# A layer norm cut into two token halves, and modulation steps moved behind their weight tiles

## The chip, the cores and the metric

The kernel runs on one core of a Trainium2 chip. The metric is the device time of one execution in microseconds (us). All arithmetic is in float32; the projections are made of matmuls on two float32r parts of each operand.

## What is computed

Two groups of tokens, 512 of a denoising step and 128 of a context, pass through two layers that share their weights. The kernel keeps them side by side as T = 640 columns, with the 1024 features in 8 chunks of 128 partitions (`kc` 0 to 7).

```python
for l in range(DEPTH):                                   # 2 layers
    sh1, sc1, ga1, sh2, sc2, ga2 = split(silu(c) @ w_ada[l] + b_ada[l])
    h = rmsnorm(x, g_attn[l]) * (1 + sc1) + sh1
    z = h @ w_in[l]     # q, k, v | gq, gk, gv, gate | zf, zb
    o_na = neighbourhood_attention(q, k, v, cache_k, cache_v, rpb)   # or context attention
    o_gla = gla_bidir(rope(gq), rope(gk), gv, lf(zf), lb(zb), state_fwd, state_bwd)
    x = x + ga1 * (concat(o_na, rmsnorm(o_gla) * silu(gate)) @ w_o[l])
    h = rmsnorm(x, g_mlp[l]) * (1 + sc2) + sh2
    x = x + ga2 * (relu(h @ w_up[l]) ** 2 @ w_down[l])
```

## The kernel before

**Weights.** Each layer's projections are cut into weight units of 128 x 1024 (512 KB): 24 of `w_in`, one small `z`, 8 of `w_o`, 32 of `w_up`, 32 of `w_down` (`dn`). `unit_order` (L377) lists them in the order of use. `prefetch` (L418) transfers them ahead on the SP queue into three buffers `wr`; ACT then rounds a unit to its high part `wh` and POOL subtracts to get the low part `wl`, each in three buffers. A unit that stands twice within four places of the list has its subtraction shared between DVE and POOL. A tile is the product of one unit with all tokens: 8 chunks, three matmuls (`wh` with the high part of h, `wh` with the low, `wl` with the high) for each of the token halves 0 to 256 and 256 to 640 (`HALF`), so 48 matmuls.

**Modulation steps.** The six modulation vectors come from products with `w_ada`, a step for each vector and chunk: `ada_step` (L498) reads a 512 KB tile of `w_ada` and makes two DVE instructions (`junk<-wr,cbc` and `wr<-wr,cbc`), one for each group's condition. In the first attention half (layer one, `adab == 1`) there are 24 of them, in the same three `wr` buffers as the weights: one each with units 6 to 23 of `w_in`, six with the first four of `w_o` (`steps_at`). In the list a step's tile stands right behind the weights of its tile. `proj` calls the step after the first chunk of that tile, `proj4` after its last evacuation. These calls give the order in which instructions are written down, not the order on DVE.

**Order.** PE's order is that of the program, made by a planner (`Drv`) that interleaves the tiles with tasks of the attention: `gla_pair`, `gv_task`, `v_task`, `qk_task`, `na_unit`. The order on the other engines is made at compile time by a scheduler, which takes instructions by priority when it reckons their inputs to be ready. An instruction without early inputs, like a step's, can so be put far ahead of its place in the program.

**The GLA chain.** `gla_pair` runs once for each pair of heads. DVE makes decay factors (`ex`), states (`ST`), masked blocks (`Dg`, `A`); PE consumes each, and PE's fixed order waits at the first that is late.

**Norm of layer two.** Every norm but the first is late: `late_begin` and `late_chunk` (L749, L762) give the projection the rows G * x, without the factor rstd, and with two shift columns more (TX = 642). The sum of squares (`sqa`) is finished meanwhile (`late_stat`), and each evacuation multiplies by `lrstd` on DVE and adds the shift's product on ACT (`whole`, and the first branches of `gla_rope`, `v_task`). Between the layers, `mlp` (L1520) does this at b == 8 for the last four `dn` units, over all tokens at once; then `late_first` (L633) starts the first two tiles of layer two and the `z` tile. The first norm of layer one is a half-token norm instead (`norm_begin`, `norm_rstd`, `norm_out`, L697 on): for each half, rstd, product `y`, scale and shift, high part on ACT, low part on POOL (or DVE). Evacuations then need neither `lrstd` nor `whole`.

## Time and profile before

| | us |
|---|---|
| median of 3 runs | 1763.83 |
| lowest, highest | 1761.66, 1766.52 |
| profiled execution | 1761.31 |
| its span | 1759.5 |
| PE busy | 1654.6 (94%) |
| DVE busy | 1087.4 (62%) |
| ACT busy | 706.4 (40%) |
| POOL busy | 606.6 (34%) |

The span runs from the first instruction to the last of one execution; its own time is 1.8 us longer. Busy time of one engine overlaps that of the others. All instructions are made by one helper, so every row has line L197, and groups are told apart by tile names: `ps_mm` and `ps_sm` are PSUM accumulators, `row` is a row of x, h or an attention output. Layer one's attention half lies from 64 to 432 us, its second norm and MLP to 913, layer two's attention half to 1274, its MLP behind that.

### The profile page before, as it was taken

What the parts mean: (1) busy time and instruction counts of PE and PEld (TensorE: products, weight loads), DVE (VectorE), ACT (ScalarE), POOL (GpSimd) and SP (SyncE); (2) the same over time, 40 slices, a digit from 0 to 9 for tenths busy, and PEclk for the clock granted to TensorE, in tenths of its full rate; (3) what the DMA queues carried; (4) which work ended last, traced back from release to release, by engine and by line L of the source; (5) the groups of instructions that cost most, each with busy time, mean ns of one, the idle gap of its engine ahead of it and who ended that gap; (6) DMA issues with size and microseconds to landing.
All of it is one profiled execution on the core that took longest, in us unless ns stands there. A gap on an engine that the chain in (4) does not pass through costs nothing. (4 is left out here: it accounts for less than half of the span.)

```text
span 1759.5 us, 32558 instructions
## 1 busy us (share of the span) xinstructions
PE 1654.6 (94%) x13708; PEld 1579.8 (90%) x13708; DVE 1087.4 (62%) x1983; ACT 706.4 (40%) x1141; POOL 606.6 (34%) x249
## 2 busy tenths in 40 slices
PE   8977687999999999999998897999999999999999
PEld 6976677779999999999998796878899999999998
DVE  5787857786697787777666766478662222222322
ACT  4525325553543233322344364467355223332330
POOL 1243522122344444444434355313133333333331
PEclk9989889999999999999999998999999999999999
DMA  9222214241354453445231111222212222222221
GB/s 367 67 88 76 85 59 149 84 133 49 108 180 145 146 178 132 144 145 167 75 132 49 42 50 57 77 66 79 77 61 84 74 83 72 73 73 83 73 72 72
DMA packets 60770, 177.18 MB, mean 101 GB/s; under 512 B 6865, under 2 KB 17745, under 8 KB 60625
## 3 DMA queue, kind: packets, MB, share of 16 engines
q1 hardware_dynamic: 44784, 157.66, 26.7%
q10 hardware_dynamic: 15840, 17.45, 3.2%
q8 instruction: 108, 1.77, 0.4%
q14 instruction: 38, 0.30, 0.1%
HBM read 168.26 MB, written 6.82 MB: 100 GB/s over the span
## 5 line engine op out<-in xcount | busy, mean ns | idle before, releaser
L197 POOL TENSOR_TENSOR wl<-wr,wh 128x1024 fp32r<-128x1024 f32 x184 | 480.7, 2613 | 922.4 <-ACT wh L197 855.5
L197 PE MATMUL ps_mm<-row,wh 128*128 128x256 f32 x2416 | 485.0, 323 | 0.8 <-POOL row L197 0.7
L197 ACT ACTIVATE wh<-wr 128x1024 fp32r<-128x1024 f32 x191 | 202.1, 1058 | 597.2 <-PE ps_sm L197 401.6
L197 PEld LDWEIGHTS ps_mm<-row,wh 128*128 128x128 f32 x2416 | 402.3, 194 | 19.8 <-issue 12.5
L197 PE MATMUL ps_mm<-row,wl 128*128 128x256 f32 (+2 forms) x1208 | 282.2, 315 | 0.5 <-DVE wl L197 0.5
L197 PEld LDWEIGHTS ps_mm<-row,wl 128*128 128x128 f32 x1208 | 227.0, 194 | 0.7 <-DVE wl L197 0.7
L197 DVE SCALAR_TENSOR_TENSOR row<-ps_mm,mod,row 128x512 f32<-128x512 f32 (+1 forms) x176 | 88.6, 543 | 89.5 <-PE ps_mm L197 89.4
L197 DVE SCALAR_TENSOR_TENSOR row<-ps_sm,mod,row 128x256 f32<-128x256 f32 (+1 forms) x216 | 81.4, 431 | 95.7 <-PE ps_sm L197 95.7
L197 DVE SCALAR_TENSOR_TENSOR ar<-ar,cbc 128x1024 f32<-128x1024 f32 x56 | 122.2, 2189 | 0.7
L197 ACT ACTIVATE r<-r 128x640 f32<-128x640 f32 (+2 forms) x192 | 112.2, 617 | 18.5 <-DVE r L197 15.0
L197 PE MATMUL ps_sm<-row,wh 128*128 128x256 f32 (+1 forms) x624 | 119.2, 310 | 0.0
L197 PE MATMUL ps_sm<-uh,wl 128*128 128x256 f32 (+1 forms) x512 | 116.5, 309 | 0.0
L197 PE MATMUL ps_mm<-uh,wl 128*128 128x256 f32 (+1 forms) x512 | 116.4, 309 | 0.0
L197 PE MATMUL ps_mm<-ul,wh 128*128 128x256 f32 (+1 forms) x512 | 116.4, 309 | 0.0
L197 PE MATMUL ps_sm<-uh,wh 128*128 128x256 f32 (+1 forms) x512 | 116.4, 309 | 0.0
L197 PE MATMUL ps_sm<-ul,wh 128*128 128x256 f32 (+1 forms) x512 | 116.4, 309 | 0.0
L197 PE MATMUL ps_mm<-uh,wh 128*128 128x256 f32 (+1 forms) x512 | 116.3, 309 | 0.0
L197 DVE TENSOR_TENSOR ul<-r,uh 128x640 fp32r<-128x640 f32 x64 | 55.1, 861 | 84.5 <-ACT r L197 84.4
L197 DVE TENSOR_TENSOR r<-ps_mm,rstd 128x642 f32<-128x642 f32 x34 | 28.1, 826 | 123.7 <-PE ps_mm L197 123.7
L197 PEld LDWEIGHTS ps_sm<-row,wh 128*128 128x128 f32 x624 | 103.3, 189 | 0.0
L197 PE MATMUL ps_mm<-m,wh 128*128 128x256 f32 (+1 forms) x544 | 102.0, 309 | 0.0
L197 PEld LDWEIGHTS ps_sm<-uh,wl 128*128 128x128 f32 x512 | 93.3, 188 | 0.0
(214 smaller groups left out, 2947.0 us busy)
## 6 DMA issues: line engine op xcount, KB each, us to landing
wr<-w_up SPq DMA_DIRECT2D x64, 512.0 KB, 3.5
wr<-w_dn SPq DMA_DIRECT2D x64, 512.0 KB, 3.5
ar<-w_ada SPq DMA_DIRECT2D x56, 512.0 KB, 3.8
wr<-w_in SPq DMA_DIRECT2D x48, 512.0 KB, 3.6
wr<-w_ada SPq DMA_DIRECT2D x24, 512.0 KB, 3.5
wa<-w_ada SPq DMA_DIRECT2D x16, 512.0 KB, 10.2
wr<-w_o SPq DMA_DIRECT2D x16, 512.0 KB, 3.5
tab<-bias ACTq DMA_DIRECT2D x32, 96.0 KB, 2.1
```

The costliest lines, as they stand in the source:

```text
L197: r = f(*args, **kw)
```

## The change

Three things change.

- In the first attention half a modulation step is called behind the last evacuation of its tile, no longer after the first chunk, and both its instructions get an ordering edge to the last matmul written down so far (`lastmm`), so that the scheduler can't put them on DVE ahead of that point. The edge makes no wait on the chip.
- Layer two's first norm becomes a half-token norm. The last four `dn` units stand twice in the list; `norm_tail` runs them for tokens 0 to 256 and then for 256 to 640. After the first pass `norm_half_task` makes the first half's rows, beside the second pass. `first_a` runs layer two's first two tiles over the first half, `first_b` the `z` tile and the second half.
- Layer two's attention half has T = 640 columns and evacuates without `lrstd` and `whole` (`lateh` is False there). `z` moves behind the first two units in the list.

```diff
--- before.py
+++ after.py
@@ -385,7 +385,7 @@
                 u.append(("ada", *next(it)))
         for l in range(L):
             for i in range(24):
-                if i == (4 if l == 0 else 0):
+                if i == (4 if l == 0 else 2):
                     put("z", l, 0)
                 put("in", l, i)
             for i in range(4):
@@ -395,6 +395,9 @@
             for b in range(9):
                 for i in range(4 if b < 8 else 0):
                     put("up", l, 4 * b + i)
+                if b == 8 and l + 1 < L:
+                    for i in range(4):
+                        put("dn", l, 4 * (b - 1) + i)
                 for i in range(4 if b > 0 else 0):
                     put("dn", l, 4 * (b - 1) + i)
         assert next(it, None) is None
@@ -502,8 +505,12 @@
         ui, t = self.unit("ada", l, v, kc)
         junk = self.junk()
         for r in range(2):
-            nc.vector.scalar_tensor_tensor(out=junk if r == 0 else t, in0=t, scalar=1.0, in1=self.cbc[:, r], op0=ALU.mult,
+            i = nc.vector.scalar_tensor_tensor(out=junk if r == 0 else t, in0=t, scalar=1.0, in1=self.cbc[:, r], op0=ALU.mult,
                                            op1=ALU.mult, accum_out=self.mod[l][:, v, kc, r:r + 1])
+            if self.adab == 1:
+                self.tc.add_manual_dep(i.ins, self.lastmm.ins.name, mybir.DependencyInfo(
+                    mybir.DependencyClass.NoSync, mybir.DependencyReason.DATA), reason="order")
         if kc == KC - 1:
             b0 = PC_BADA + 48 * l + 8 * v
             m = self.mod[l][:, v]
@@ -543,22 +550,22 @@
         for i, (w, h) in enumerate(((wh, hh), (wh, hl), (wl, hh))):
             for hf in halves:
                 lo = self.HALF[hf][0]
-                nc.tensor.matmul(ps[0][hf], lhsT=w, rhs=h[:, lo:lo + ps[0][hf].free_size()],
+                self.lastmm = nc.tensor.matmul(ps[0][hf], lhsT=w, rhs=h[:, lo:lo + ps[0][hf].free_size()],
                                  start=first and i == 0 and (hf == 1 or shared is None),
                                  stop=last and i == 2 and (hf == 1 or shared in (None, 1)))
         self.dv.pe(sum((0.32, 0.48)[hf] for hf in halves))
 
-    def mmz(self, ps, w):
-        for kc in range(KC):
-            hh, hl = self.h[kc]
-            for m, h in ((64, hh), (32, hl)) if kc < KC - 1 else ((32, hl), (64, hh)):
-                for hf in range(2):
-                    lo = self.HALF[hf][0]
-                    self.nc.tensor.matmul(ps[0][hf][0:m], lhsT=w[:, kc, 0:m], rhs=h[:, lo:lo + ps[0][hf].free_size()],
+    def mmz(self, ps, w, halves=(0, 1)):
+        for hf in halves:
+            lo, hi = self.HALF[hf]
+            for kc in range(KC):
+                hh, hl = self.h[kc]
+                for m, h in ((64, hh), (32, hl)) if kc < KC - 1 else ((32, hl), (64, hh)):
+                    self.nc.tensor.matmul(ps[0][hf][0:m], lhsT=w[:, kc, 0:m], rhs=h[:, lo:hi],
                                           start=kc == 0 and m == 64, stop=kc == KC - 1 and m == 64)
-        self.dv.pe(4.7)
+            self.dv.pe((1.9, 2.8)[hf])
 
     def mmf(self, f, kc, halves, shared=None):
         ui, ps, w = f
@@ -594,7 +601,7 @@
         ps, nsm = self.acc_any(n=n)
         for kc in range(KC):
             self.mm3(ps, wh[:, kc], wl[:, kc], *self.h[kc], kc == 0, kc == KC - 1)
-            if kc == 0:
+            if kc == 0 and self.adab > 1:
                 self.ada_at(*key)
             if kc < KC - 1:
                 yield
@@ -602,6 +609,8 @@
         with self.tc.high_priority(offset=self.EVP):
             evac(ps[1])
         self.acc_done(ps, nsm)
+        if self.adab == 1:
+            self.ada_at(*key)
         yield
 
     def first_steps(self, keys):
@@ -630,29 +639,37 @@
         for f in self.firsts:
             self.used(f[0])
 
-    def late_first(self, l, keys):
-        uz, wz = self.unit("z", l, 0)
-        fs = []
+    def first_a(self, l, keys):
+        self.firsts = []
         for key in keys:
             ui, w = self.unit(*key)
-            fs.append((ui, self.acc(TX), self.split_k(w)))
+            self.firsts.append((ui, self.acc(), self.split_k(w)))
+        for kc in range(KC):
+            for f in self.firsts:
+                self.mmf(f, kc, (0,))
+            yield
+    def first_b(self, l, evacs):
+        uz, wz = self.unit("z", l, 0)
+        ps = self.acc_sm()
+        self.mmz(ps, wz, (0,))
         for kc in range(KC - 2):
-            for f in fs:
-                self.mmf(f, kc, (0, 1))
+            for f in self.firsts:
+                self.mmf(f, kc, (1,))
             yield
-        ps = self.acc_sm(TX)
-        self.mmz(ps, wz)
+        self.mmz(ps, wz, (1,))
         self.used(uz)
-        self.first_evacs[0](ps[1])
-        self.dv.rel("sm", 2, self.est.free(*(p[0] for p in ps[1])))
+        evacs[0](ps[1])
+        self.dv.rel("sm", 2, 1.5)
         yield
-        for n, f in enumerate(fs):
+        for n, f in enumerate(self.firsts):
             for kc in range(KC - 2, KC):
-                self.mmf(f, kc, (0, 1))
+                self.mmf(f, kc, (1,))
             self.used(f[0])
             with self.tc.high_priority(offset=self.EVP):
-                self.first_evacs[1 + n](f[1][1])
+                evacs[1 + n](f[1][1])
             yield
 
     def z_tile(self, l, evac):
@@ -701,6 +718,33 @@
         self.nsum = [False, False]
         self.nready = [False, False]
         self.rstd = npl.tile([128, T], F32, name="rstd", bufs=1)
+    def norm_chunk(self, x, kc, hf):
+        nc, p = self.nc, self.npl
+        lo, hi = self.HALF[hf]
+        if kc == hf == 0:
+            self.sqa = p.tile([128, T], F32, name="sqa", bufs=1)
+        acc = self.sqa[:, lo:hi]
+        if kc == 0:
+            nc.scalar.activation(out=acc, in_=x[kc][:, lo:hi], func=AF.Square)
+        else:
+            sq = p.tile([128, 384], F32, name="sq")[:, 0:hi - lo]
+            nc.scalar.activation(out=sq, in_=x[kc][:, lo:hi], func=AF.Square)
+            if kc < KC - 1:
+                nc.vector.tensor_tensor(out=acc, in0=acc, in1=sq, op=ALU.add)
+        if kc == KC - 2:
+            self.dv.spawn(self.norm_sum(hf, acc, True), self.est.until(acc))
+        elif kc == KC - 1:
+            self.dv.spawn(self.norm_sum(hf, sq, False), self.est.until(acc, sq))
+    def norm_sum(self, hf, sq, first):
+        lo, hi = self.HALF[hf]
+        self.nc.tensor.matmul(self.nss[hf][:, 0:hi - lo], lhsT=self.ones, rhs=sq, start=first, stop=not first)
+        self.dv.pe((0.43, 0.64)[hf])
+        if not first:
+            self.nsum[hf] = True
+        yield 0.0
 
     def norm_rstd(self, hf):
         lo, hi = self.HALF[hf]
@@ -740,6 +784,36 @@
         eng = nc.vector if kc < 3 and hf == 0 else nc.gpsimd
         eng.tensor_tensor(out=hl[:, lo:hi], in0=y[:, :n], in1=hh[:, lo:hi].bitcast(F32), op=ALU.subtract)
 
+    def norm_half_task(self, l, which, x, hf, rows):
+        while not self.nsum[hf]:
+            yield 0.4
+        if hf == 0:
+            self.norm_scale(l, which)
+            self.h = rows
+        self.norm_rstd(hf)
+        for kc in range(KC):
+            self.norm_out(l, which, x, kc, hf, rows, hf == 0)
+            if hf == 0 and kc < KC - 1:
+                yield 1.5
+        self.nready[hf] = True
+    def norm_tail(self, l, which, x, vec, lw, kind, units, act, rows):
+        dv = self.dv
+        self.rot = True
+        for hf in range(2):
+            for j, i in enumerate(units):
+                def ev(m, ps):
+                    self.resid(lw, vec, x, 2 * j + m, ps, (hf,))
+                    if which == 0:
+                        if hf == 1:
+                            self.nc.scalar.dma_start(out=self.xs[2 * j + m], in_=x[2 * j + m])
+                    self.norm_chunk(x, 2 * j + m, hf)
+                self.filler(self.proj4((kind, lw, i), act, ev, (hf,)))
+            dv.spawn(self.norm_half_task(l, which, x, hf, rows))
+        self.rot = False
+        dv.until(lambda: self.nready[0])
     def pair_rows(self, reg, i, n=T):
         return self.row(reg, 2 * i, F32R, n), self.row(reg, 2 * i + 1, F32R, n)
 
@@ -797,10 +871,10 @@
         win = iter(range(24))
         nxt = lambda: ("in", l, next(win))
         if l > 0:
-            first = self.late_first(l, [nxt(), nxt()])
-            self.filler(islice(first, KC - 2))
-            dv.until(lambda: self.lready)
+            self.filler(self.first_a(l, [nxt(), nxt()]))
+        dv.until(lambda: self.nready[1])
+        if l > 0:
             self.mlp_ctx.close()
         with self.pool(f"att{l}", reuse_waits="tile") as ap:
             self.ap = ap
@@ -835,8 +909,7 @@
                     dv.rel("sm", 2, 2.0)
                     self.filler(self.z_tile(l, z_evac))
                 else:
-                    self.first_evacs = [z_evac] + [lambda segs, i=i: self.gla_rope(l, 0, i, segs) for i in range(2)]
-                    self.filler(first)
+                    self.filler(self.first_b(l, [z_evac] + [lambda segs, i=i: self.gla_rope(l, 0, i, segs) for i in range(2)]))
                 for h in range(2 if l == 0 else 0, 4):
                     dv.take("gt")
                     self.filler(self.proj(nxt(), lambda ps: self.start(self.gv_task(h, ps))))
@@ -1541,18 +1614,10 @@
                 adac.close()
                 self.adap = None
                 npl = self.mlp_ctx.enter_context(self.pool(f"norm1_{l}", 2, reuse_waits="tile"))
-                rows = [self.pair_rows((self.reg[0], self.reg[2])[i // 4], i % 4, TX) for i in range(8)]
-                self.h = rows
-                self.late_begin(l + 1, 0, npl, rows)
-                def ev_x(m, ps):
-                    kc = 2 * j + m
-                    self.resid(l, 5, x, kc, ps)
-                    nc.scalar.dma_start(out=self.xs[kc], in_=x[kc])
-                    self.late_chunk(x, kc, rows)
-                for j in range(4):
-                    self.filler(self.proj4(("dn", l, 28 + j), prev, ev_x))
-                self.rot = False
+                rows = [self.pair_rows((self.reg[0], self.reg[2])[i // 4], i % 4) for i in range(8)]
+                self.norm_begin(npl)
+                self.norm_tail(l + 1, 0, x, 5, l, "dn", range(28, 32), prev, rows)
+                self.lateh = False
             elif b > 0:
                 for j in range(4):
                     self.filler(self.proj4(("dn", l, 4 * (b - 1) + j), prev, ev4(j)))
```

## Rows read from the trace of the kernel before

**Rows 1.** Stretches: busy us of PE, PEld, DVE, ACT, POOL; PEclk is TensorE's granted clock.
```profile
64.00:254.00 190.00, 149.42 (x2052) 134.31 (x2051) 153.77 (x221) 72.98 (x116) 73.66 (x26) 0.89 0.25 80
254.00:432.00 178.00, 160.70 (x1181) 140.73 (x1180) 129.50 (x347) 86.87 (x186) 42.27 (x20) 0.94 0.32 103
432.00:879.00 447.00, 446.46 (x3036) 445.88 (x3035) 350.46 (x509) 160.56 (x219) 184.22 (x64) 1.00 0.42 141
...
933.00:1122.00 189.00, 162.91 (x2174) 149.31 (x2173) 128.43 (x185) 87.41 (x134) 83.69 (x34) 0.94 0.16 49
1122.00:1274.00 152.00, 145.63 (x1136) 129.23 (x1136) 108.36 (x309) 88.56 (x187) 36.20 (x17) 0.99 0.27 82
```

**Rows 2.** What PE waited for, 80 to 440 us: us in total, times, longest.
```profile
PE ps_sm L197 <- DVE ST L197: 14.2, 2, 8.0
PE ps_sm L197 <- DVE A L197: 12.0, 2, 6.9
PE ps_sm L197 <- DVE kT L197: 5.2, 1, 5.2
...
PE ps_sm L197 <- ACT gt L197: 1.1, 1, 1.1
```

**Rows 3.** Timeline of DVE, 236 to 247 us: start, us, instruction, idle before and releaser.
```profile
241.20 1.23 DVE L197 SCALAR_TENSOR_TENSOR junk<-wr,cbc 128x1024 bf16<-128x1024 f32 x1 [5.14 <-DMA wr<-w_ada]
...
244.08 2.05 DVE L197 COPY_PREDICATED A<-masks,Dg 32x320 f32<-32x320 int32 x4
```

**Rows 4.** Timeline of PE, 239.5 to 247 us.
```profile
246.18 1.22 PE L197 MATMUL ps_sm<-A,gv 128*128 128x128 f32 x4 [5.07 <-DVE A L197]
```

**Rows 5.** Timeline of the SP queue, 230 to 246 us.
```profile
236.52 0.33 SPq L197 DMA_DIRECT2D wr<-w_ada  x1
```

**Rows 6.** DVE groups, 60 to 440 us: count, busy us, mean ns, idle before them.
```profile
L197 DVE SCALAR_TENSOR_TENSOR junk<-wr,cbc 128x1024 bf16<-128x1024 f32 x24 | 42.1, 1754 | 27.9 <-DMA wr<-w_ada 27.9
...
L197 DVE SCALAR_TENSOR_TENSOR wr<-wr,cbc 128x1024 f32<-128x1024 f32 x24 | 34.0, 1416 | 0.4
```

**Rows 7.** The page's DMA issues: count, KB each, median us to landing.
```profile
wr<-w_ada SPq DMA_DIRECT2D x24, 512.0 KB, 3.5
```

**Rows 8.** The page's costliest groups: the two halves of a weight tile's split.
```profile
L197 POOL TENSOR_TENSOR wl<-wr,wh 128x1024 fp32r<-128x1024 f32 x184 | 480.7, 2613 | 922.4 <-ACT wh L197 855.5
...
L197 ACT ACTIVATE wh<-wr 128x1024 fp32r<-128x1024 f32 x191 | 202.1, 1058 | 597.2 <-PE ps_sm L197 401.6
```

**Rows 9.** The chain that ended last: the 48 matmuls of one full tile.
```profile
1325.12 7.07 PE ps_sm L197 x48
```

**Rows 10.** What PE waited for, 940 to 1300 us.
```profile
PE ps_sm L197 <- ACT gt L197: 13.2, 3, 4.8
```

**Rows 11.** DVE groups, 925 to 1300 us: the products with the late norm's rstd.
```profile
L197 DVE TENSOR_TENSOR raw<-ps_mm,rstd 128x642 f32<-128x642 f32 x8 | 6.6, 823 | 6.2 <-PE ps_mm L197 6.2
L197 DVE TENSOR_TENSOR tmp<-ps_mm,rstd 128x642 f32<-128x642 f32 x8 | 6.6, 821 | 9.2 <-PE ps_mm L197 9.2
L197 DVE TENSOR_TENSOR gt<-ps_mm,rstd 128x512 f32<-128x512 f32 x4 | 4.3, 1075 | 0.7 <-PE ps_mm L197 0.6
```

**Rows 12.** Timeline of DVE, 906 to 921 us, where layer one ends.
```profile
907.64 2.33 DVE L197 SCALAR_TENSOR_TENSOR row<-row,G,row 128x128 fp32r<-128x128 f32 x1 [0.16 <-ACT row L197]
...
919.32 0.81 DVE L197 TENSOR_TENSOR sqa<-sqa,sq 128x640 f32<-128x640 f32 x1
```

**Rows 13.** Timeline of PE, 912 to 927 us: last w_down matmuls, then the norm's sums.
```profile
912.80 0.46 PE L197 MATMUL ps_sm<-uh,wl 128*128 128x256 f32 x2
...
920.19 1.34 PE L197 MATMUL ps_ss<-sqa,ones 128*128 128x256 f32 x4 [1.61 <-DVE PN L197]
```

**Rows 14.** Groups, 20 to 66 us: the half-token norm at the start, layer one.
```profile
L197 POOL TENSOR_TENSOR row<-y,row 128x384 fp32r<-128x384 f32 x8 | 10.0, 1265 | 30.4 <-ACT row L197 30.4
...
L197 DVE TENSOR_TENSOR y<-row,rstd 128x384 f32<-128x384 f32 x8 | 6.7, 832 | 1.5 <-POOL row L197 0.9 <-ACT rstd L197 0.6
...
L197 DVE TENSOR_SCALAR y<-y,G,mod 128x256 f32<-128x256 f32 x8 | 2.9, 410 | 0.1
```

## The prediction

> **What bounds the kernel now.** I read the busy times by stretch first [rows 1]. In layer one's MLP (432 to 879 us) PE is busy 446.5 of 447 us, and no edit touches that stretch. The two attention halves are where time can be won: from 64 to 432 us PE is idle for 40.6 + 17.3 = 57.9 us and its granted clock is 0.89 and 0.94, from 933 to 1274 us it is idle for 26.1 + 6.4 = 32.5 us at 0.94 and 0.99. Both run the same attention; the first has 24 modulation steps more, the second has the late norm's evacuations. No engine is full there (DVE 154 of 190 us at the most), so the bound is a chain of waits, and the next view to read is what PE waited for. In the first half 14.2 + 12.0 + 5.2 = 31.4 us stand behind DVE, in five waits for `ST`, `A` and `kT` [rows 2]. In the second half the largest item is ACT's `gt`, 13.2 us in three waits [rows 10], where the first half shows 1.1 us [rows 2].
>
> One wait, followed back, shows how the first half loses its time. PE stands for 5.07 us until `A` is there [rows 4]. DVE makes `A` from 244.08 on, but before that it had been idle for 5.14 us with a modulation step at the head of its queue, whose `w_ada` tile had not landed [rows 3]. That tile was issued at 236.52 [rows 5], so the step stood on DVE before its data was even on the way. Over the half, DVE is idle 27.9 us in front of the 24 first instructions of the steps, all of it waiting for `w_ada`, and the 48 instructions take 42.1 + 34.0 us themselves [rows 6].
>
> **Part one: the steps go behind their tiles.** What goes is the wait for data. The tile of a step stands in the list behind its own weights, whose matmuls have then all been written down; the three `wr` buffers let it be loaded some two tiles ahead, and a tile is 7.07 us of PE [rows 9] against 3.5 us to landing [rows 7]. What stays is the work: 24 times two instructions, 1.23 us each where nothing disturbs them [rows 3], the second like the first in shape [rows 6]: 2.46 us a step. It no longer lies where the scheduler finds a hole, but behind an evacuation, so it still stands in front of some instruction of the GLA chain. I take it that each of the five large waits keeps one step, 5 x 2.46 = 12.3 us, of its 31.4 us: a gain of 19 us. The ends: 31 us, where no step stands in front of the chain any more, and nothing, where the chain meets other late links at once.
>
> The clock follows. At 0.89 over 190 us it is worth 0.05 x 190 = 9.5 us of elapsed time less than at the 0.94 of the second half's GLA stretch, itself with idle PE [rows 1]. PE idles a third less, so I take a third, 3 us; the ends are 0 and 9.
>
> The move also has a price. A step's execution frees its `wr` buffer, and the weights three units on wait for that buffer. From the step to usable weights it takes 2.46 + 3.5 [rows 7] + 1.06 + 2.61 [rows 8] = 9.6 us. There are two tiles of cover, 14.1 us [rows 9]; this holds while DVE executes the step less than 4.5 us behind the end of its tile. In `w_o` the cover is thinner: two steps stand behind one tile, 12.1 us to the second-next weights, covered by one tile and the neighbourhood tasks between. I take 2 us of PE wait at each of two such tiles, 4 us in all; ends 0 and 15. Together part one gives -19 - 3 + 4 = -18 us.
>
> **Part two: layer two's attention without the late factors.** The products with `rstd` go: 6.6 + 6.6 + 4.3 us for 20 of the tiles [rows 11], with ACT's bias passes behind them; an ACT copy from PSUM takes their place, one link fewer between PE and the transposes. What this is worth is read at the transposes that wait for `gt`: 13.2 us with the product [rows 10], 1.1 us with the copy alone in the first half [rows 2], where ACT does the same work. 12.1 us is the upper end of that wait. The copy must still queue behind ACT's exponentials, and the chain behind it has other links (`ksT` among them), so I take two thirds: -8 us. The lower end is 0. Two columns fewer in each tile are worth 2 of 642, under 0.03 us for 7.07 us, and are left out.
>
> **Part three: the boundary.** The `dn` work itself is unchanged: two passes of 256 and 384 columns have the same matmuls and columns as one of 640. Four more units are loaded and split; with three units held ready and 2.8 us of PE work in each of the short passes (0.4 x 7.07), POOL would be late with 2.61 us a unit and other work, but the sharing with DVE roughly halves that, and I cost it at nothing; if this cover is gone, PE waits about 1 us at each of four units. What counts is the tail. Before, the last `dn` matmul starts at 913.0 and DVE finishes the squares at 920.13 [rows 12, 13]: 7 us of backlog, hidden by the first two tiles but for 1.61 us [rows 13]. After, the second half's norm can begin only when its last column is in. Its 8 chunks cost DVE 0.83 for the product and about 2 x 0.41 for two scalings [rows 14], a little much since the second is on 128 columns: 1.65 us each, 13.2 us; POOL's 1.27 us [rows 14] lies beside it. Evacuation, square, sum and rstd ahead of them I estimate at 3 us, from the 1.34 us of the four sums [rows 13] and as many short ACT and DVE instructions. The last chunk is usable 3 + 13.2 + 1.3 = 17.5 us after the last matmul, plus DVE's backlog, and some 2 us of PE work follow: 19.5 us. PE itself has two tiles, the `z` tile (32 matmuls, 4.7 us by rows 9) and the sums: 14.1 + 4.7 + 1.3 = 20.2 us, today 21.8 with the wait. Without backlog the boundary thus gains 1.6 us; with the 7 us of today it ends at 26.5 and loses 5. The first half's rows are made in the second pass, where DVE is about as loaded as today, so the backlog is nearer to today's: +3 us; ends -2 and +12.
>
> The shared engines could make this worse. A DVE instruction on 128 columns took 2.33 us while POOL split weights, one on 640 columns 0.81 us later on [rows 12]; `y` took 0.83 on average beside POOL's subtractions [rows 14]. The Trainium skill says in "SBUF — State Buffer", section "SBUF: two separate sides", that DVE with two SBUF inputs and POOL share a port pair as an exclusive lock, the later one blocked for the whole instruction. The rows agree with it in kind; it speaks against this part, since `y` and the low parts then take turns. What that would cost is the second rival.
>
> **The sum.** -18 - 8 + 3 = -23 us on the profiled 1761.3 us, 1738. The median of the runs shown is 2.5 us above that execution, so 1741 us.
>
> **Rivals.**
> - The GLA chain is slow in itself: the steps still stand in front of it wherever they are put, and the removed `gt` waits turn into waits for `ST`, `A` and `ksT`. For it: DVE is 81% busy from 64 to 254 us, and 48 instructions remain [rows 1, 6]. Against it: the second half has fewer such waits with the same chain. Part one gives 6 us, part two 4: 1764 - 6 - 4 + 3 = 1757.
> - `y` and the low parts take turns at the boundary: 0.83 + 0.82 + 1.27 = 2.9 us a chunk, 23 us for eight, 10 more than above; half of `dn`'s second pass can suffer too. 1741 + 9 = 1750. By the rule cited above this would be the likeliest; the mean of 0.83 against 1.27 for POOL says that `y` is seldom blocked for a whole instruction.
> - Part one comes out in full, -31 - 6 with no wait in `w_o`: 1764 - 37 - 8 + 3 = 1722.
> - Slower: the steps starve the weights. In the first attention half DVE runs steps 7 us behind their tiles, 2.5 over the 4.5 that the cover allows, and the weights three units on come late at 14 of the 24 places. That is 35 us, and PE's waits are for `wl` and `wh`: 1741 + 35 = 1776. It decides at 4.5 us of lag. For it: DVE's stretches without a hole are several us long; against it: where DVE is fullest, tiles are spread over more than 7 us by the tasks between them.
> - The edge does not do what it says, since other instructions without early inputs still stand ahead: part one gives nothing, 1764 - 8 + 3 = 1759.
>
> **Chances.** The forecast 0.48 (1730 to 1755), the chain 0.13, the turns 0.12, the full gain 0.10, slower 0.12, no effect of the edge 0.05. A measurement of this kernel tells about 0.3% from no change, 1758.5 to 1769.1. Faster: 0.48 + 0.12 + 0.10 and 0.08 of the chain's, 0.78; slower 0.12; the rest, 0.10, is the same. The range runs from 1724 to 1764: it leaves out the slower case and half of the full gain.
>
> **What would show it.** Part one is right if DVE's idle time before `junk<-wr,cbc` falls from 27.9 us to under 5, and PE's waits for `ST`, `A` and `kT` fall to some 12 us; it is wrong if waits for `wl` or `wh` stand among PE's. Part two: PE's wait for `gt` after the boundary under 5 us. Part three: PE's idle time between the last `dn` matmul and the second tile's end, 1.61 us now, at 2 to 8 us; if it is over 10, the turns were the case. A span of the first attention half that doesn't shrink would make the forecast wrong.

## The result and the profile after

The changed kernel takes 1745.79 us (median; 1743.11 to 1747.37), the kernel before 1762.74 beside it: a ratio of 0.9892 [0.9869, 0.9916], 17 us faster. The forecast was 1741 us in [1724, 1764], faster with 0.78. The profiled execution's span is 1743.6 us, 1759.5 before.

The total came out, but its terms did not. I cut both traces at five marks: the first `z` matmul (64.9 us after, 64.0 before), DVE's first reading of an `up` tile of layer one, the end of the last `dn` matmul of the passes that feed the norm, the first `tmp` evacuation of layer two, and the first `up` tile of layer two; what follows is 443.0 to 444.1 us everywhere. The stretches between them, us of each profiled execution, with the result of each run:

```
run        median   ratio to before          A attention 1  B MLP 1  C boundary  D attention 2
before     1762.74                           410.4          438.9    20.1        383.0
after      1745.79  0.9892 [0.9869, 0.9916]  402.1          442.5    29.9        361.2
e_steps    1752.24  0.9925 [0.9910, 0.9940]  400.7          438.9    19.8        382.0
e_norm     1757.71  0.9956 [0.9938, 0.9973]  413.2          444.1    30.3        356.8
e_noedge   1749.21  0.9910 [0.9894, 0.9925]  404.1          444.1    30.8        360.9
e_kc0      1739.89  0.9850 [0.9831, 0.9869]  398.4          442.5    30.5        362.6
e_link     1766.73  1.0004 [0.9992, 1.0016]  402.4          442.5    29.7        382.7
e_act      1744.62  0.9880 [0.9861, 0.9900]  404.3          442.5    30.7        359.4
e_o        1746.78  0.9893 [0.9872, 0.9913]  404.9          444.1    30.3        361.0
e_nobuf    1746.02  0.9882 [0.9855, 0.9908]  392.7          444.1    30.4        356.3
e_small    1716.78  0.9728 [0.9702, 0.9753]  371.0          442.5    29.9        360.7
e_split    1742.49  0.9873 [0.9850, 0.9895]  402.2          442.5    27.9        362.2
e_late     1743.59  0.9867 [0.9849, 0.9885]  398.5          442.5    30.8        359.9
e_best     1735.95  0.9818 [0.9798, 0.9839]  395.4          442.5    28.0        361.1
```

From before to after: A -8.3, B +3.6, C +9.8, D -21.8, the start +0.9; with -0.1 behind the last mark that is -15.9 us, the difference of the spans. The forecast had -18 for A, nothing for B, +3 for the boundary, -8 for D.

**The first attention half.** Stretch A as a whole (columns as in [rows 1]), first of before, then of after:

```profile
64.00:474.30 410.30, 351.88 (x3511) 316.23 (x3510) 311.96 (x614) 179.67 (x333) 127.96 (x51) 0.93 0.28 92
...
64.90:467.00 402.10, 352.56 (x3512) 314.81 (x3511) 309.95 (x614) 181.10 (x333) 123.11 (x51) 0.94 0.29 94
```

Over the whole of A, PE and DVE do the same work as before; PE idles for 49.5 us instead of 58.4. What PE waited for between 80 and 440 us in after, against [rows 2], and the steps on DVE, against [rows 6]:

```profile
PE ps_mm L197 <- POOL sqo L197: 7.3, 2, 5.4
PE ps_sm L197 <- ACT ksT L197: 7.2, 1, 7.2
PE ps_mm L197 <- DVE sql L197: 5.8, 4, 2.8
PE ps_sm L197 <- DVE ex L197: 4.0, 1, 4.0
...
PE ps_sm L197 <- DVE kT L197: 1.8, 1, 1.8
...
PE ps_sm L197 <- DVE ST L197: 1.1, 1, 1.1
...
PE ps_sm L197 <- DVE A L197: 1.0, 1, 1.0
```

```profile
L197 DVE SCALAR_TENSOR_TENSOR wr<-wr,cbc 128x1024 f32<-128x1024 f32 x24 | 41.3, 1720 | 0.6
L197 DVE SCALAR_TENSOR_TENSOR junk<-wr,cbc 128x1024 bf16<-128x1024 f32 x24 | 32.2, 1344 | 0.1
```

DVE's idle time for `w_ada` is gone (27.9 to 0), and so are PE's waits for `ST`, `A` and `kT` (31.4 to 3.9 us). But four other waits, 24.3 us, now lead the list: `sqo` (squares of the GLA output, made on POOL) and `ex` are new, `ksT` (transposed scaled keys, copied from PSUM on ACT) was 3.4 us before and `sql` (low part of the squares of q and k) 4.3.

**Layer two.** PE's wait for `gt` from 925 to 1290 us, against [rows 10]; then the mark between C and D, the first `tmp` evacuation, in after (a copy on ACT, where before has a product with `rstd` on DVE [rows 11]):

```profile
PE ps_sm L197 <- ACT gt L197: 1.2, 1, 1.2
```

```profile
939.42 0.68 ACT L197 ACTIVATE tmp<-ps_mm 128x640 f32<-128x640 f32 x1
```

Stretch D of before, of after and of the run `e_link` below, which puts the evacuations' links back:

```profile
933.40:1316.40 383.00, 350.05 (x3586) 319.47 (x3585) 265.48 (x541) 195.45 (x351) 131.93 (x56) 0.96 0.21 64
...
939.40:1300.60 361.20, 343.56 (x3576) 314.00 (x3575) 240.42 (x511) 181.67 (x330) 136.29 (x56) 0.98 0.22 68
...
938.60:1321.30 382.70, 349.81 (x3580) 319.49 (x3580) 264.61 (x538) 196.46 (x352) 132.98 (x56) 0.96 0.20 64
```

In D both parts of PE's time fall: its idle time by 15.3 us (33.0 to 17.6) and its busy time by 6.5, at a granted clock of 0.98 instead of 0.96.

**The boundary.** PE in after, against [rows 13]; DVE's additions of squares and POOL's split beside the last of them, against [rows 12]; and the two stretches of 7 us around the start of the tiles (columns as in [rows 1]):

```profile
893.31 0.70 PE L197 MATMUL ps_ss<-sqa,ones 128*128 128x256 f32 x2 [2.75 <-DVE sqa L197]
...
912.06 0.47 PE L197 MATMUL ps_mm<-row,wh 128*128 128x256 f32 x2 [2.18 <-DVE row L197]
...
916.36 1.65 PE L197 MATMUL ps_ss<-sqa,ones 128*128 128x384 f32 x2 [2.33 <-DVE sqa L197]
```

```profile
911.83 0.55 DVE L197 TENSOR_TENSOR sqa<-sqa,sq 128x384 f32<-128x384 f32 x1
...
913.90 2.40 DVE L197 TENSOR_TENSOR sqa<-sqa,sq 128x384 f32<-128x384 f32 x1 [0.87 <-ACT sq L197]
```

```profile
913.53 2.36 POOL L197 TENSOR_TENSOR wl<-wr,wh 128x1024 fp32r<-128x1024 f32 x1 [2.69 <-ACT wh L197]
```

```profile
905.00:912.00 7.00, 4.88 (x30) 4.67 (x28) 6.80 (x12) 2.40 (x4) 3.16 (x2) 1.00 0.48 178
912.00:919.00 7.00, 4.61 (x17) 3.74 (x18) 5.47 (x7) 5.21 (x12) 4.16 (x3) 0.53 0.67 238
```

PE waits 2.18 us for the first half's rows; in the 7 us from the end of this wait on, in which it waits 2.33 us more for the squares, the granted clock is 0.53, near the lower level of 1.2 GHz.

### The profile page after: what moved, and what is told of

Read it like the earlier page. It is cut to its first block, busy times and chain, and to the rows that moved or that the text cites. A ratio compares the mean times of both kernels' runs of the same rounds, so it can differ in the third digit from the quotient of the medians.

```text
span 1743.6 us, 32610 instructions
## 1 busy us (share of the span) xinstructions
PE 1653.4 (95%) x13712; PEld 1575.1 (90%) x13712; DVE 1076.4 (62%) x1971; ACT 703.3 (40%) x1142; POOL 626.7 (36%) x266
## 5 line engine op out<-in xcount | busy, mean ns | idle before, releaser
L197 POOL TENSOR_TENSOR wl<-wr,wh 128x1024 fp32r<-128x1024 f32 (+1 forms) x188 | 490.1, 2608 | 906.0 <-ACT wh L197 856.5
L197 PE MATMUL ps_mm<-row,wh 128*128 128x256 f32 (+1 forms) x2416 | 485.8, 322 | 7.9 <-DVE row L197 3.7
L197 ACT ACTIVATE wh<-wr 128x1024 fp32r<-128x1024 f32 x195 | 206.3, 1058 | 627.7 <-PE ps_sm L197 400.7
L197 DVE SCALAR_TENSOR_TENSOR row<-ps_mm,mod,row 128x128 f32<-128x128 f32 (+2 forms) x180 | 89.4, 536 | 79.2 <-PE ps_mm L197 79.0
L197 DVE TENSOR_TENSOR r<-ps_mm,rstd 128x642 f32<-128x642 f32 x34 | 28.1, 827 | 123.7 <-PE ps_mm L197 123.7
L197 DVE SCALAR_TENSOR_TENSOR r<-ar,cbc 128x1024 bf16<-128x1024 f32 x56 | 93.6, 1689 | 0.0
```

Of the source, the lines that this page charges most:

```text
L197: r = f(*args, **kw)
```

## The experiments

**One part alone.** `e_steps` is the kernel before with part one only, `e_norm` the changed kernel with the steps as before, `e_noedge` the changed kernel without the edge but with the step called behind its tile.

> The kernel before with the modulation steps moved and ordered as in the change, the norm of layer two left as it was. Theory (the parts add up as the landmarks of the changed trace read): first attention half 8 us shorter, all else as before, 1763 - 8 = 1755 us; DVE's idle time for w_ada under 3 us. Rival (the prediction's own term): 1763 - 18 = 1745 us, the gain of the steps having been eaten elsewhere by the norm.

> The changed kernel with the modulation steps called and ordered as before: layer two's half-token norm alone. Theory: boundary 12 us longer, layer two's attention 20 us shorter, 1763 - 8 = 1755 us, DVE idle for w_ada 25 to 30 us. Rival (the prediction's terms): -8 + 3, 1758 us, and 17 us of difference to the changed kernel must then come from the steps.

> The changed kernel with the ordering edge taken out, the steps still called behind their tiles. Theory (the edge does it): the steps are put ahead again, DVE idles 20 us or more for w_ada, first attention half within 3 us of the one before, total 1754 us. Rival (the later place in the program is enough): no idle time for w_ada, 1746 us.

```
 # e_norm, e_noedge: the changed kernel without
-            if self.adab == 1:
-                self.tc.add_manual_dep(i.ins, self.lastmm.ins.name, ...)
 # e_norm also
-            if kc == 0 and self.adab > 1:
+            if kc == 0:
                 self.ada_at(*key)
...
-        if self.adab == 1:
-            self.ada_at(*key)
```

Part one alone gives 0.9925, the norm alone 0.9956; the product, 0.988, is the whole. In the table part one acts only on A (-9.7), the norm on B, C and D (its A, +2.8, has nothing changed in it and shows what one execution is good for). Without the edge DVE still idles 20.0 us for `w_ada`:

```profile
L197 DVE SCALAR_TENSOR_TENSOR junk<-wr,cbc 128x1024 bf16<-128x1024 f32 x24 | 40.4, 1681 | 20.1 <-DMA wr<-w_ada 20.0
```

and PE's waits for `ST`, `A` and `kT` between 80 and 440 us stand at 26.0 us, against 31.4 in before and 3.9 in after:

```profile
PE ps_sm L197 <- DVE ST L197: 11.2, 2, 6.1
PE ps_sm L197 <- DVE A L197: 8.9, 2, 7.6
PE ps_sm L197 <- DVE kT L197: 5.9, 2, 5.3
```

Yet the time is 0.991, an interval that overlaps with after's, and A is 6.3 us shorter than before's. So behind its tile the step hardly needs the edge: 20 us of DVE's idle time and 22 us of named waits are worth about 2 us of A, no more than one execution is good for. Neither of the two outcomes expected came as a whole.

**The place of the step.** `e_kc0` keeps the edge, but the step is called behind the first of its tile's eight chunks, as before.

> The changed kernel with the steps called after the first chunk of their tile as before, but with the edge. Theory (what counts is that a step is not put ahead of its data): no idle time for w_ada and 1744 to 1748 us. Rival (the place behind the evacuation counts): the step stands in front of its tile's evacuation and the GLA chain, 1750 us or more.

```
-            if kc == 0 and self.adab > 1:
+            if kc == 0:
                 self.ada_at(*key)
...
-        if self.adab == 1:
-            self.ada_at(*key)
```

0.985: 4 us shorter in A than after, and the intervals only touch. The step some 6 us of PE work earlier (seven of eight chunks of a tile, [rows 9]) is the better place; `e_best` and `e_split` below, which differ only in this place, confirm it with intervals that do not overlap. Against `e_norm`, from which it differs only by the edge, A is 15 us shorter: called early, the step needs the edge, called late it hardly does. `e_o` takes the edge from the six steps of `w_o` alone (`if self.adab == 1 and self.edge`, false for `o` tiles).

> The changed kernel without the edge for the six steps of w_o, so that they may be put ahead; the eighteen of w_in keep it. Theory (the neighbourhood stretch lost 10 us to steps that now fall into it): that stretch gets 3 to 5 us back, 1742 us, with some idle time for w_ada. Rival (what it lost is the PE order, not the steps): 1746 us.

No change (0.9893), so the edge in `w_o` is not what A lacks.

**Gone or only moved?** The steps' instructions alone, by stretch; behind the length stand the busy times of PE and PEld (0 here) and of DVE, then PE's granted clock. The cuts are the first `z`, the first `A,gv`, the first `kT,qT` and the last `pT,V` matmul of layer one. Before, then after:

```profile
64.00:153.00 89.00, 0.00 (x0) 0.00 (x0) 28.75 (x32) 0.92 0.28 89
153.00:288.40 135.40, 0.00 (x0) 0.00 (x0) 30.49 (x36) 0.89 0.26 86
288.40:424.50 136.10, 0.00 (x0) 0.00 (x0) 17.16 (x28) 0.93 0.31 98
```

```profile
65.00:140.00 75.00, 0.00 (x0) 0.00 (x0) 8.68 (x12) 0.98 0.21 68
140.00:271.20 131.20, 0.00 (x0) 0.00 (x0) 29.13 (x37) 0.88 0.27 90
271.20:414.30 143.10, 0.00 (x0) 0.00 (x0) 30.04 (x41) 0.94 0.31 97
```

20 us of step work left the first stretch, which became 14 us shorter; 13 us came to the neighbourhood stretch, which became 7 us longer. Two kernels test this. `e_late` moves four more steps from tiles 6 to 9 to tiles 20 to 23; `e_small` keeps every tile and wait but lets the 48 instructions work on 64 of 1024 columns.

> The changed kernel, but four of the modulation steps stand later: none behind tiles 6 to 9 of layer one's attention, two instead of one behind tiles 20 to 23. In the changed kernel the stretch from the `z` tile to the first `A,gv` matmul holds 7 instructions of the steps, 9.9 us (16 and 28.7 us before the change), and takes 75.1 us (89.0 before); the neighbourhood stretch, from the first `kT,qT` to the last `pT,V` matmul, holds 20 and 30.2 us (14 and 17.1 before), and takes 143.0 us (136.0 before). Theory one (the edge for a good part only moves DVE's step work from the first stretch to the later ones, and PE's waits go with it, about 0.7 us of time for 1 us of steps in both): the first stretch falls to 70 to 72 us, the neighbourhood stretch with the `w_o` tiles grows by 4 to 7 us, the whole is the same or up to 4 us slower: 1745 to 1750. Theory two (the first stretch gained because data no longer is waited for, and the steps themselves are covered in either place): the first stretch stays at 74 to 76, the neighbourhood stretch at 142 to 144, 1746.

```
-            return (0, 0, 0, 0, 0, 0, 1, 1, 1, 1, 1, ..., 1, 1, 1, 1)[i]
+            return (0, 0, 0, 0, 0, 0, 0, 0, 0, 0, 1, ..., 2, 2, 2, 2)[i]
```

```profile
63.90:132.50 68.60, 0.00 (x0) 0.00 (x0) 0.00 (x0) 1.00 0.18 59
132.50:254.10 121.60, 0.00 (x0) 0.00 (x0) 24.27 (x33) 0.93 0.27 89
254.10:416.70 162.60, 0.00 (x0) 0.00 (x0) 44.30 (x64) 0.93 0.35 118
```

The first stretch falls to 68.6 us, the neighbourhood stretch grows by 19.5, more than expected, and the middle one shrinks by 10, which I had not expected; what is left of A behind them goes from 52.7 to 45.6 us. The whole is 0.9867, not to be told from after. Half of the 19.5 us is PE work that now falls into the neighbourhood stretch, as its rows for all instructions show, of after, then of `e_late`:

```profile
271.20:414.30 143.10, 127.58 (x955) 107.42 (x954) 117.72 (x309) 71.20 (x161) 28.05 (x12) 0.94 0.31 97
...
254.10:416.70 162.60, 137.29 (x1003) 115.72 (x1002) 135.60 (x347) 73.64 (x164) 34.27 (x15) 0.93 0.35 118
```

PE's idle time, which is free of that, changes by -4.9, -5.4, +9.8 and -2.6 us in the four stretches, and the step work by -8.7, -4.9, +14.3 and -6.0. Idle time goes where the steps go.

> The changed kernel, but the 48 instructions of the first attention half's 24 modulation steps work on 64 of their 1024 columns: tiles are loaded and buffers held as before, DVE is relieved of some 70 us, and layer one's later modulation vectors are not those of the reference. Theory one (late freed buffers): with nothing to execute the buffers come free at the end of their tile, ACT's wait for `wr<-w_in` falls below 10 us, and the gain holds both what the buffers cost (6 to 12 us) and what DVE's work costs in the chain. Theory two (DVE's work alone): the gain here is the whole price of the steps, 10 to 20 us, and the kernel without buffers held gains nothing. If this one gains no more than 3 us over the other, DVE's work itself is hidden.

```
+            n = 64 if self.adab == 1 else 1024
-            i = nc.vector.scalar_tensor_tensor(out=junk if r == 0 else t, in0=t, ...
+            i = nc.vector.scalar_tensor_tensor(out=(junk if r == 0 else t)[:, :n], in0=t[:, :n], ...
```

```profile
L197 DVE SCALAR_TENSOR_TENSOR wr<-wr,cbc 128x64 f32<-128x64 f32 x24 | 12.7, 529 | 0.9
L197 DVE SCALAR_TENSOR_TENSOR junk<-wr,cbc 128x64 bf16<-128x64 f32 x24 | 8.7, 363 | 0.1
```

```profile
63.50:434.50 371.00, 341.06 (x3512) 306.30 (x3511) 250.43 (x615) 180.38 (x333) 116.93 (x51) 0.97 0.31 102
```

1716.78 us, 29 less than after, all in A (-31.1). DVE is relieved of 73.5 - 21.4 = 52.1 us, so a microsecond of step work still costs 0.60 us of A on average, where the change has put it. That is the mechanism of the chain rival, which gave part one 6 us. Of the 31.1 us, 19.6 are PE's idle time (49.5 to 29.9) and 11.5 its busy time (352.6 to 341.1), at a granted clock of 0.97 instead of 0.94.

**Late buffers.** In after ACT waits 30.5 us in ten places between 80 and 440 us for `wr<-w_in`, a wait that is not in before's list. One of them, on ACT, PE and DVE of after:

```profile
ACT wh L197 <- DMA wr<-w_in: 30.5, 10, 7.4
```

```profile
174.50 3.96 DVE L197 SCALAR_TENSOR_TENSOR wr<-wr,cbc 128x1024 f32<-128x1024 f32 x1
```

```profile
181.87 1.06 ACT L197 ACTIVATE wh<-wr 128x1024 fp32r<-128x1024 f32 x1 [5.09 <-DMA wr<-w_in]
182.83 0.58 ACT L197 ACTIVATE ksT<-ps_sm 128x512 f32<-128x512 f32 x1
```

```profile
183.47 1.76 PE L197 MATMUL ps_sm<-gv,ksT 128*64 128x128 f32 x14 [7.16 <-ACT ksT L197]
```

The step ends at 178.4 and frees the `wr` buffer, the transfer is issued at 178.49, the weights land at 181.87, and `ksT`, for which PE stands, queues behind their copy on ACT. The time that the steps take is not by itself what makes the weights late: in `e_small`, where they take 21.4 us instead of 73.5, I had expected this wait to fall below 10 us, and it grew, although A is 31 us shorter:

```profile
ACT wh L197 <- DMA wr<-w_in: 38.6, 15, 6.0
```

`e_nobuf` lets the steps read the constant `cbc`, so that they hold no buffer.

> The changed kernel, but the 24 modulation steps of the first attention half read the constant `cbc` instead of their `w_ada` tiles: the tiles are not loaded and hold no `wr` buffer, and layer one's later modulation vectors are therefore not those of the reference. DVE's 48 instructions stay. In the changed kernel ACT's `wh` copies wait 30.5 us for `wr<-w_in` and 8.5 us for `wr<-w_o` between 80 and 440 us, 0 in the kernel before. Theory one (a step executed late frees its `wr` buffer late, the next weights are issued late, and ACT stands in its queue for them with `ksT` and `sqo` behind): those 39 us go to under 3, PE's waits for `ksT` and `sqo` between 80 and 440 us fall from 14.5 us to under 6, the first half ends 6 to 12 us earlier, 1734 to 1740. Theory two (the steps cost what DVE needs for them, the buffers nothing): ACT's waits move to other names, the time stays within 3 us of the changed kernel's 1746.

```
-                                t = self.wp.tile([128, 1024], F32, name="wr", ...)
-                            nc.sync.dma_start(out=t, in_=self.a["w_ada"][l, v, kc])
+                                t = None
...
+                  in0=self.cbc[:, 1 - r] if t is None else t, ...
```

```profile
L197 DVE SCALAR_TENSOR_TENSOR junk<-cbc 128x1024 bf16<-128x1024 f32 x48 | 87.8, 1830 | 0.4
```

ACT's wait for `wr<-w_in` vanishes, PE's waits for `ksT` and `sqo` fall from 14.5 to 3.4 us as expected, those for `sql` and `ST` grow from 6.9 to 14.2, and the time is 1746.0 as in after. That does not settle it: the same 48 instructions took 87.8 instead of 73.5 us, 17 instead of 10 of them over 1.5 us, and at 0.60 the 14.3 us would hide 8.6 us, about the gain expected. Its six executions also lie between 1732.6 and 1747.2, and the profiled one is the shortest, so its row of the table is no measure. What late buffers cost stays open between 0 and some 9 us.

**The late factors.** `e_link` puts the links back in layer two: a product with a tile of ones on DVE and a bias pass with a column of zeros on ACT.

> The changed kernel with the links of the late evacuations put back in layer two's attention: each evacuation multiplies by a tile of ones on DVE and adds a column of zeros on ACT, so values are unchanged; norm and boundary stay as changed. Theory (layer two's attention gained its 20 us from the removed links): 1746 + 20 = 1766 us, PE's wait for gt back at 10 us or more. Rival (the gain came from the boundary's other start, tasks lying differently): 1746 to 1752 us.

```
-        if self.lateh:
+        if self.link:
...
+                self.link = True
+                nc.vector.memset(self.lrstd[:, 0:T], 1.0)
```

```profile
PE ps_sm L197 <- ACT gt L197: 8.6, 2, 5.8
PE ps_sm L197 <- ACT ksT L197: 5.5, 1, 5.5
```

The whole gain of the change is gone (1.0004), and D is 382.7 again: its idle time (32.9 us), its busy time and its clock are those of before. The links are worth 21 us. The wait for `gt` came back to 8.6 us, less than the 10 expected, and still D is as long as before.

**The boundary.** `e_act` puts the two scalings of the second half's odd chunks on ACT; `e_split` makes the low parts of the first three `in` weights of layer two on DVE instead of POOL.

> The changed kernel with the scaling of the second half's odd chunks on ACT in place of DVE at the boundary. Theory (DVE's 1.85 us a chunk, blocked by POOL, sets the second half's norm): four chunks lose about 0.9 us each of DVE time, the second tile of layer two ends 3 us earlier, 1743 us. Rival (POOL's low parts set it, 1.0 us and their waits): unchanged, 1746 us.

> The changed kernel, but the low parts of the first three `in` weights of layer two are made on DVE instead of POOL. In the changed kernel POOL makes them at 903, 908 and 913 us, 2.40 us each, and a DVE addition of squares that starts in the same moment takes 2.45, 2.45 and 2.40 us instead of the 0.54 of the others; the last of the three ends at 916.3 and the sum over the squares waits for it. Theory one (POOL's splits hold the boundary): the three additions take 0.55 us, the second half's norm begins 2 to 4 us earlier against the last `dn` matmul (11.9 us now), and the distance from the last `dn` matmul to the end of the second tile falls from 30.1 us to 26 to 28; 1742 to 1744. Theory two (the boundary is held by the amount of DVE and ACT work): DVE's own 3 x 1.1 us take what the blocked additions took, the distance stays within 1 us of 30, no change from 1746.

```
 # e_act
-            self.norm_out(l, which, x, kc, hf, rows, hf == 0)
+            self.norm_out(l, which, x, kc, hf, rows, hf == 0 or kc % 2 == 1)
 # e_split
-                    if self.wx is not None:
+                    if self.wx is not None or self.units[j] in [("in", 1, 0), ("in", 1, 1), ("in", 1, 2)]:
```

Moving the scalings does nothing (C 30.7). Moving the splits does what was expected of it, at the lower end (from the last `dn` matmul to the end of the second tile 28.1 us instead of 30.1); the groups on DVE from 895 to 936 us, and the same two stretches of 7 us as above:

```profile
L197 DVE TENSOR_TENSOR wl<-wr,wh 128x1024 fp32r<-128x1024 f32 x3 | 3.7, 1217 | 0.0
L197 DVE TENSOR_TENSOR sqa<-sqa,sq 128x384 f32<-128x384 f32 x6 | 3.3, 547 | 0.0
```

```profile
905.00:912.00 7.00, 5.64 (x36) 5.23 (x34) 7.00 (x16) 4.89 (x10) 0.00 (x0) 1.00 0.87 316
912.00:919.00 7.00, 6.80 (x46) 5.91 (x47) 1.48 (x4) 4.26 (x11) 3.55 (x5) 1.00 0.29 92
```

The additions take 0.55 us, the low clock is gone, and C is 27.9, 2 us less. The median, 3 us under after's, agrees, though the two intervals overlap. What holds the second half's norm now is PE's own order. The last addition ends 2.9 us behind the last `dn` matmul, at 911.73, but PE comes to the sum of the squares only at 916.21, without an idle moment right before it, since matmuls of layer two's first tiles stand ahead of it in its queue:

```profile
911.18 0.55 DVE L197 TENSOR_TENSOR sqa<-sqa,sq 128x384 f32<-128x384 f32 x1
...
916.21 0.81 PE L197 MATMUL ps_ss<-sqa,ones 128*128 128x384 f32 x2
```

**Both together.** `e_best` has the edits of `e_kc0` and `e_split`.

> The changed kernel with two edits of earlier runs together: the step is written down behind the first of its tile's eight chunks, as before the change, but keeps its edge; and the low parts of the first three `in` weights of layer two are made on DVE. The first alone gave 0.985 of the kernel before, the second 0.9873, the changed kernel 0.9892. If the two are independent (one in layer one, one at the boundary), 0.983: 1735 us beside 1765 of before. If the gain of the first is one of the spread of the granted clock from run to run (its spans were 1731 to 1741), 0.986 to 0.988.

1735.95 us, 0.9818 [0.9798, 0.9839]: it is faster than before and than after, whose interval does not overlap with its own, and the product of the two edits (0.983) lies in its interval. A is 395.4 and C 28.0.

## Why the prediction was right, and where its terms were not

- **Part one, -18, came as -8.3 in A.** What I had named as the signs happened in full: idle time 27.9 to 0, the three waits 31.4 to 3.9 (I had expected some 12). But for a step called behind its tile little of the gain hangs on them: `e_noedge` has 20.0 and 26.0 us of them and a time close to after's. The step that failed is the one that turned the fall of named waits into time ("keeps one step, 12.3 of its 31.4 us"). The waits fell by more than the 19 us that I took, and PE's idle time in A by 8.9; a step on DVE then stood right in front of `sql`, where PE waited longest for it (357.4 to 362.0 us), and late weights held ACT's queue in front of `ksT` and `sqo`. I had shown that the work stays and did not ask who stands behind it in its new place.
- **The clock, -3, gave nothing.** PE was busy for 351.9 us of A before and for 352.6 after, with a granted clock of 0.93 and 0.94. The gain from the clock came elsewhere: 6.5 us of PE's busy time in D, for which the sum had no term.
- **The weights, +4.** Their waits came, not as PE's waits for `wl` or `wh`, which I had named as the sign, but in ACT's queue in front of `ksT`. Their price is open.
- **Part two, -8, came as -21.8.** The wait for `gt` fell by 12.0 us, the upper end; I had taken two thirds, because I expected `ksT` behind it to keep the rest, but PE's wait for `ksT` vanished too (5.7 us before). Together with small waits that grew, PE's idle time in D fell by 15.3 us. The other 6.5 us are its busy time at the higher clock (ten of the 3586 matmuls lie on the other side of the mark). `e_link` shows the 21 us as a whole; it puts the product on DVE and the pass on ACT back together, so it stays open how much is the shorter way from PE to the transposes and how much the 17.5 us of products [rows 11] that left DVE.
- **Part three, +3.** By the measure of the text, the end of the second tile behind the last `dn` matmul, 21.7 us became 30.1: +8.4, within the ends of -2 and +12; PE's idle time in it is 6.7 us, inside the 2 to 8 that were to show part three. The norm of the second half begins 11.9 us behind the last matmul (3 + 7 = 10 with the full backlog), its eight chunks take 14.8 us with POOL's last subtraction (13.2 + 1.3), and PE ends 3.4 us later (2 taken). The backlog was as today's, where I had taken less: the additions end 6.8 us behind the last `dn` matmul. But it was made by POOL's splits, which held three of them, and behind it came a term that the sum did not have, PE's order: in `e_split`, with a backlog of 2.9 us, the norm still begins at 10.1. The turns rival, 2.9 us a chunk, did not come: a chunk takes 1.74 in the steady state (3.47 for two, their products starting at 927.17 and 930.64).
- **The eight short passes, costed at nothing, took 3.6 us in B.** POOL kept up, and PE waits for no weights there, as I had reckoned; but PE stands 2.75 us in front of the first half's sum of squares, which is in its queue between the passes.

By the marks of the table the errors are +10 in A, +4 in B, +7 in C and -14 in D; they cancel but for 7, and the span fell by 15.9 instead of 23 us. That the total came out within 5 us is luck: it rests on two errors of 10 us and more that cancel, and D alone is past the 12 us that I had given as its upper end. `e_link` shows how near it was: without the gain of the links the time would have been that of before.

## What to carry to other kernels

A wait that vanishes from PE's list is not time: compare PE's idle time over the whole stretch, and count the work that was moved in the stretch where it now lies. Where a chain of short tasks runs through one engine that is three quarters busy, the work on that engine counts as much as its place: here 52 us less of it brought 31 us, and the best place found for it 15 (`e_best`). Look at the clock as well: where PE stood idle for less, its busy time fell too in D (6.5 us) and in A of `e_small` (11.5), though not in A of after. In an in-order queue a wait that one engine loses can reappear on another: look for the buffer that is now freed later, and for what stands behind the instruction that waits for it.

## What the runs showed of the hardware

- The DVE additions of two SBUF tensors that begin 0.4 us into a POOL subtraction of weights last until 0.4 us behind its end: 2.40 us beside POOL's 2.36 (913.90 and 913.53 us), 0.55 without it. The Trainium skill states this in "SBUF — State Buffer", section "SBUF: two separate sides", as an exclusive lock; row and rule agree. It is not always DVE that waits: the product `y` of two SBUF tensors at 924.14 takes 0.55 us, although a POOL subtraction runs from 923.81 on, and there it is the subtraction that is long, 1.75 us against 1.05 for the next. That scalings with one SBUF tensor are held up too I had not expected (the section names DVE's two-port modes beside two inputs; no row shows in which mode these ran):

```profile
922.51 1.24 DVE L197 TENSOR_SCALAR y<-y,G,mod 128x256 f32<-128x256 f32 x4
...
924.61 2.64 DVE L197 TENSOR_SCALAR y<-y,G,mod 128x256 f32<-128x256 f32 x4
```

  Four of them take 1.24 us with POOL idle and 2.64 with POOL's subtractions beside the first two.
- The same low part of 128x1024 takes POOL 2.40 us and DVE 1.22 (`e_split`), so at this place, where the two engines held each other up, DVE alone was the cheaper one (2 us of C).
